# Attention: when the keys and values of the later blocks are asked for

## The chip, the cores and the metric

The kernel runs on one core of a Trainium2 chip. The metric is the device time of one launch in microseconds. Three runs of the kernel before took 2055.99, 2061.31 and 2060.2 us; their median is 2060.2 us.

The engines of a core work side by side, each through its own list of instructions in order: TensorE (PE) multiplies, VectorE (DVE), ScalarE (ACT) and GpSimd (POOL) do the elementwise work, SyncE (SP) mostly starts DMAs. They wait for each other by semaphores. An instruction that waits holds up all that stands behind it on its engine.

## The reference

One step of a two-layer encoder over 2048 prompt tokens and 32 sampled tokens, width 1024. The first layer is a gated delta rule, the second an attention with a sliding window over whole blocks of 64 tokens. Only the second is touched here:

```
proj = x @ w_in                                  # queries (16 heads of 64) and gates
q = rope(proj[:, :1024]) * 64 ** -0.5
kb, vb = band(k), band(v)                        # for each block: two blocks back and its own
s = einsum('bnqkgd,bnskd->bnkgqs', q, kb)        # 4 key heads, 4 query heads to each
s = where(key_chunk >= 0, s, -inf)
p = exp(s - m) / (sum(exp(s - m)) + exp(sink - m))   # m: the largest of the row and its sink
o = einsum('bnkgqs,bnskd->bnqkgd', p, vb)
out = layer_norm(alpha * x + (o * silu(z)) @ w_out)
```

Keys and values are one shared set, projected once from the output of the first layer. A block n reads the keys and values of blocks n-2, n-1 and n; block 0 reads one, block 1 two. The sampled tokens read a cache and their own keys.

## The kernel before, in words

The work of the last part: class P2 has projected keys, values, queries and gates for all tokens and has stored them in DRAM (scratch tensors `bk`, `bv`, `bq`, `bz`). Class Attention reads them back. Its loop `run` takes one block of 64 queries at a time, called a unit here; i counts the units. The order is blocks 8 to 31, then 0 to 7, then the sampled tokens, so unit i is block i + 8 for i below 24. It begins with block 8, since the projections of the last tokens are not done yet: their products (the generator `gates`, called by `fill`, two halves of a product at a time; lines 1714 to 1716) are mixed into the first units as filling work for PE.

A unit on PE is: products of probabilities with values (`values`, line 2098), the scores of the unit two ahead for one half of the heads (`scores`, line 2065), the transposes of the next unit's probabilities (line 2080), the output product of a finished pair of blocks (lines 1157 to 1159, weights `wo`), and the same for the other half of the heads. Between scores and transposes stand the maximum on DVE (line 1880), the exponentials on ACT (line 1885), the reciprocal on DVE (line 1889) and the product of the two on POOL (line 1899, tile P). The first output product is in unit 3, since a pair of blocks has to be finished first.

All keys lie in one tile `kT` (128 partitions, 2 x 2048 numbers: 16 KB a partition) and all values in one tile `vd` (two copies of 64 partitions for the two head halves). `load_keys(a, z)` is one DMA for blocks a to z - 1 (line 1847), `load_values(a, z)` two (line 1853). A block costs 64 KB of keys and 64 KB of values. Blocks 6 to 11 are loaded ahead of the loop, blocks 12 to 31 in step m = 4 of `gates`, which falls ahead of unit 0, and blocks 0 to 5 in `opened`, in unit 2.

In this stage the order on all five engines, SP's too, is written by hand (`manual_schedule` with PE, DVE, Activation, Pool and SP): what stands first in the program is issued first. On SP's list stand, beside the key and value loads: the last fetches of projection weights (line 1389), the rotary tables (1764), the stores of projected rows and gates (1747, 1740) and the regrouping of the rows (1751), the output weights `wo` in three parts (1826: four ahead of unit 0, one in unit 0, three in `opened`), the queries of a pair of blocks (`start`, line 2043, two DMAs), its gates (`gate`, 2048), the residual rows (1909) and the stores of the output (1962). From unit 4 on, each even unit has a `start`, a `gate`, a residual row and, when one is ready, an output store; odd units had no DMA.

Three places matter for the change: the loads in `gates` and in `opened`, and the top of the loop in `run`.

Of the kernel before, what the change touches and what calls it, by code (L numbers as in the profile page):

```python
# [36 lines left out]
def new_pool(tc, es, name, bufs=1, space=None, side=None):  # L37
    kw = {"reuse_waits": "tile"}
    if side is not None:
        kw["side"] = side  # L40
    if space is not None:
        kw["space"] = space
    return es.enter_context(tc.tile_pool(name=name, bufs=bufs, **kw))
# [49 lines left out]
def drain(gen):  # L93
    for _ in gen:
        pass
# [530 lines left out]
class Delta:  # L626
# [366 lines left out]
    LOADS = "Lk", "LE", "Lq0", "Lq1"  # L993
# [330 lines left out]
class P2:  # L1324
# [8 lines left out]
    FETCH, SUM, CAST, SUB, STEPS = 12, 5, 3, 2, 2  # L1333
    EARLY, LATE = 4, 2
    HELD, MORE = 5, 3
# [3 lines left out]
    def __init__(self, tc, right, front, spare, I, O, T, G):  # L1339
# [9 lines left out]
        self.ppr = new_pool(tc, spare, "p2_psr", 2, PSUM, side="right")  # L1349
        self.slots = self.EARLY + self.LATE  # L1350
        self.sub = self.nc.gpsimd
# [443 lines left out]
class Attention:  # L1795


    EARLY = 4
    LATE = 5

    def __init__(self, tc, left, I, O, T, G):
        self.tc, self.nc, self.I, self.O, self.T, self.G = tc, tc.nc, I, O, T, G
# [29 lines left out]
    def middle_weights(self, left):  # L1832
        return self.weights(new_pool(self.tc, left, "t_wo2", 1, side="left"), self.EARLY, self.LATE)

# [6 lines left out]
    def load_late(self):  # L1841
        drain(self.weights(self.oone, self.LATE, KC))
        yield
        self.tabs = ln_tables(self.nc.sync, self.oone, self.I["b_ln_g"], self.I["b_ln_b"])
# [270 lines left out]
    def run(self, gates, opened):  # L2115

        order = list(range(8, 32)) + list(range(8))
        last = len(order)
        P, pts, soft = {}, {}, {}
        gate = iter(gates)  # L2120

        def fill(n):
            for _ in range(n):
                next(gate, None)

        def score(i, p):
            if i <= last:
                P[i, p], soft[i, p] = self.scores(order[i], p) if i < last else self.sampled_scores(p)

        def sinks(i, p):  # L2130
            if i < last:
                self.place_sinks(p, 2, self.keys(order[i])[1] * 64, p * 4)
            elif i == last:
                self.place_sinks(p, 1, 160, 8 + 2 * p)

        def largest(i, p):
            if i <= last:
                self.largest(soft[i, p])

        def exps(i, p):  # L2140
            if i <= last:
                self.exps(soft[i, p])
                sinks(i + 1, p)

        def shares(i, p):
            if i <= last:
                x = soft.pop((i, p))
                self.inverse(x)
                self.shares(x)

        def turn(i, p):
            x = P.pop((i, p))
            pts[i, p] = self.turned(order[i], x) if i < last else self.sampled_turned(x)

        def copies(i, p):
            if i < last:
                self.copies(order[i], *pts[i, p])
            else:
                self.sampled_copies(*pts[i, p])

        def got(i):
            return [pts.pop((i, p))[0] for p in range(2)]

        norm = [None, None]

        def step(n):
            for _ in range(n if norm[1] else 0):
                next(norm[1], None)

        def early(i, p):  # L2170
            score(i, p)
            largest(i, p)
            exps(i, p)

        sinks(0, 0)
        sinks(0, 1)
        fill(4)
        early(0, 0)
        fill(2)
        shares(0, 0)  # L2180
        early(0, 1)
        fill(2)
        shares(0, 1)
        early(1, 0)
        turn(0, 0)
        copies(0, 0)
        fill(2)
        turn(0, 1)
        copies(0, 1)
        shares(1, 0)  # L2190
        score(1, 1)
        po = done = following = stored = None
        for i in range(last):
            c = (i + 1) % 2
            if i >= 3 and c == 0:
                done, po = po, following
            if i == 1:
                self.start(order[6])
            elif i == 2:
                self.gate(order[6])  # L2200
            elif i % 2 == 0:
                if i + 4 < last:
                    self.start(order[i + 4])
                    self.gate(order[i + 4])
                if i + 4 == last:
                    self.sampled_keys()
            if i == 2:
                fill(1)
            banks = self.values(order[i], got(i))
            gated = self.gated(order[i], banks, c)  # L2210
            largest(i + 1, 1)
            exps(i + 1, 1)
            drain(gated)
            score(i + 2, 0)
            turn(i + 1, 0)
            copies(i + 1, 0)
            largest(i + 2, 0)
            exps(i + 2, 0)
            shares(i + 1, 1)
            if i < 2:  # L2220
                fill(2)
            if po:
                self.product(po, c, 0)
            old = None
            if i >= 4:
                x = po if c else done
                if x:
                    self.stats(x, 1 - c)
                    if c == 0:
                        old = norm[0]  # L2230
                        step(20)
                        norm[:] = x, self.norm(x)
            step(4)
            shares(i + 2, 0)
            step(5)
            if c == 1 and i >= 2:
                following = self.finish(*self.pend.pop(0)) if i > 2 else opened()
                self.cast(following)
                self.rest(following)
            if old:  # L2240
                self.normed(old)
                self.affine(old)
                stored = old
            elif stored:
                self.store(stored)
                stored = None
            if po:
                self.product(po, c, 1)
                self.added(po, c)
            turn(i + 1, 1)  # L2250
            copies(i + 1, 1)
            score(i + 2, 1)
        self.store(stored)
        old = norm[0]
        step(20)
        self.normed(old)
        self.pend.append(self.sampled_values(got(last)))
        final, sampled = self.pend
        self.product(po, 1, 0)
        self.stats(po, 0)  # L2260
        some = self.finish(*sampled)
        self.cast(some)
        self.rest(some)
        self.affine(old)
        self.product(po, 1, 1)
        self.added(po, 1)
        self.stats(po, 1)
        end = self.finish(*final)
        self.cast(end)
        self.rest(end)  # L2270
        self.store(old)
        drain(self.norm(po))
        self.normed(po)
        self.affine(po)
        for c in range(2):
            self.product(some, c, 0)
            self.product(some, c, 1)
            self.added(some, c)
            self.stats(some, c)
        self.store(po)  # L2280
        for c in range(2):
            self.product(end, c, 0)
            self.product(end, c, 1)
            if c == 0:
                drain(self.norm(some))
                self.normed(some)
                self.affine(some)
                self.store(some)
            self.added(end, c)
            self.stats(end, c)  # L2290
        self.tail(end)
# [20 lines left out]
def program(tc, I, O, T, G):  # L2312
# [108 lines left out]
    att = Attention(tc, left, I, O, T, G)  # L2421
    later.append(att)

    def gates():
        for m in range(14):
            next(p2.main)
            next(p2.main)
            if m == 4:
                att.load_keys(12, 32)
                att.load_values(12, 32)  # L2430
                early = att.early_weights()
            elif m == 6:
                next(early)
            elif m == 8:
                drain(early)
            elif m == 10:
                front.close()
                drain(att.middle_weights(left))
            yield
        drain(p2.main)  # L2440
        p2.finish_all()
        yield

    def opened():
        right.close()
        att.open_right(right)
        late_weights = att.load_late()
        next(late_weights)
        first = att.finish(*att.pend.pop(0))
        drain(late_weights)  # L2450
        att.load_keys(0, 6)
        att.load_values(0, 6)
        return first

    with tc.manual_schedule(engines={ET.PE, ET.DVE, ET.Activation, ET.Pool, ET.SP}):
# [165 lines left out]
```

## Time and profile before

| | |
|---|---|
| median of three runs | 2060.2 us (2055.99 to 2061.31) |
| the profiled execution | 2062.93 us, its span 2061.1 us |
| PE busy | 1998.8 us, 97% of the span |
| PE weight loads busy | 1826.2 us (beside the products) |
| DVE, ACT, POOL busy | 1471.9, 1000.2, 748.0 us |
| DMA | 377.85 MB, 183 GB/s on average |

A profile is one execution. A row of the timeline gives the start in us, the length, engine, line, operation, the tiles written and read, how many were merged, and in brackets the idle time of the engine ahead of it and who ended that. "SPq" rows are SP's issues of DMAs: their length is the time that SP needs to hand the DMA over, not that of the transfer. A row of a window gives the stretch, its length, busy time of PE, PE's weight loads, DVE, ACT and POOL (number of instructions in brackets), the granted clock of PE, the busy share of the 16 DMA engines (it can go above 1, since packets overlap) and GB/s.

### The profile page before, as it was taken

The numbers are of one execution on the slowest core, as the hardware profiler recorded it, in microseconds if no ns is written. First come the engines' busy times: TensorE is split into PE (matmuls) and PEld (weight loads), VectorE is DVE, ScalarE is ACT, GpSimd is POOL, SyncE is SP. The second block draws the span as 40 slices with busy tenths as digits, with TensorE's granted clock in tenths as the row PEclk, the third lists the DMA queues.
The fourth block names the chain that finished last, engine by engine and source line by source line (L and its number), as shares of the span: only waits on it lengthen the run. The fifth ranks groups of instructions, "written<-read, shape, count | busy, mean of one in ns | idle before, by whom it ended". The sixth has DMA issues, their size and how long they took to land. (4 is left out here: it accounts for less than half of the span.)

```text
span 2061.1 us, 36534 instructions
## 1 busy us (share of the span) xinstructions
PE 1998.8 (97%) x13246; PEld 1826.2 (89%) x13246; DVE 1471.9 (71%) x2701; ACT 1000.2 (49%) x2437; POOL 748.0 (36%) x1151
## 2 busy tenths in 40 slices
PE   8999999999999999999889999899999998999998
PEld 6999999999999999999788887799999996777775
DVE  4567656677666778888987998777777654666665
ACT  4354444436632277777763222534643435555552
POOL 0412112112223258888860123022000023566665
PEclk9999999999999999999999999999999999999999
DMA  5134255447878566666884989888768579433321
GB/s 211 48 116 126 72 128 124 104 97 207 208 164 242 152 202 217 197 206 196 299 277 131 268 254 255 279 259 298 259 200 247 184 225 310 121 103 103 103 74 67
DMA packets 477077, 377.85 MB, mean 183 GB/s; under 512 B 291024, under 2 KB 397808, under 8 KB 476880
## 3 DMA queue, kind: packets, MB, share of 16 engines
q1 hardware_dynamic: 437136, 356.88, 57.7%
q10 hardware_dynamic: 39760, 18.64, 3.4%
q8 instruction: 104, 1.70, 0.3%
q14 instruction: 77, 0.63, 0.1%
HBM read 244.06 MB, written 142.58 MB: 188 GB/s over the span
## 5 line engine op out<-in xcount | busy, mean ns | idle before, releaser
L79 PE MATMUL ps<-act_hi,w_hi 128*128 128x416 f32 x1280 | 455.7, 356 | 4.0 <-DVE z L579 3.7
L81 PE MATMUL ps<-act_hi,w_lo 128*128 128x416 f32 x1280 | 450.5, 353 | 0.0
L80 PE MATMUL ps<-act_lo,w_hi 128*128 128x416 f32 x1280 | 448.9, 351 | 0.0
L79 PEld LDWEIGHTS ps<-act_hi,w_hi 128*128 128x128 f32 x1280 | 240.8, 188 | 9.3 <-DVE z L579 4.0
L81 PEld LDWEIGHTS ps<-act_hi,w_lo 128*128 128x128 f32 x1280 | 240.6, 188 | 3.8
L80 PEld LDWEIGHTS ps<-act_lo,w_hi 128*128 128x128 f32 x1280 | 241.1, 188 | 3.0
L212 DVE SCALAR_TENSOR_TENSOR y<-R,convw,y 128x2083 f32<-128x2083 f32 x72 | 175.5, 2438 | 57.5 <-ACT y L209 46.5
L56 POOL TENSOR_TENSOR w_lo<-w_raw,w_hi 128x1024 fp32r<-128x1024 f32 x25 | 72.3, 2891 | 275.7 <-ACT w_hi L55 275.1
L755 POOL TENSOR_TENSOR tm<-L,Tt 128x60 f32<-128x60 f32 (+19 forms) x365 | 134.8, 369 | 73.2 <-issue 43.0
L1885 ACT ACTIVATE e<-S,nm 128x193 f32<-128x193 f32 (+2 forms) x260 | 104.8, 416 | 102.8 <-DVE nm L1880 62.0
L757 POOL TENSOR_TENSOR Tt<-Tt,tm 128x60 f32<-128x60 f32 (+19 forms) x365 | 140.0, 383 | 28.6
L1899 POOL TENSOR_TENSOR P<-e,sm 128x384 f32<-128x384 f32 (+2 forms) x128 | 102.5, 823 | 123.4 <-DVE sm L1889 117.3
L326 ACT COPY R<-ps 128x416 f32<-128x416 f32 (+1 forms) x144 | 59.7, 445 | 125.5 <-PE ps L81 119.9
L1542 ACT ACTIVATE o<-X 128x416 f32<-128x416 f32 x80 | 41.5, 519 | 144.8 <-PE X L1716 141.6
L1383 POOL TENSOR_TENSOR wo_parts<-wo_parts 128x512 fp32r<-128x512 f32 x16 | 21.4, 1341 | 240.8 <-ACT wo_parts L1703 240.8
L1157 PE MATMUL ot<-wo,g_hi 128*128 128x512 f32 x256 | 103.9, 406 | 1.8 <-DMA wo<-s_wob 1.8
L1383 DVE TENSOR_TENSOR w_lo<-w_raw,w_hi 128x512 fp32r<-128x512 f32 x134 | 95.8, 729 | 7.7 <-ACT w_hi L1395 5.9
L1158 PE MATMUL ot<-wo,g_hi 128*128 128x512 f32 x256 | 100.8, 394 | 0.0
L1159 PE MATMUL ot<-wo,g_lo 128*128 128x512 f32 x256 | 100.8, 394 | 0.0
L1430 POOL TENSOR_TENSOR act_raw<-act_raw 128x416 f32<-128x416 f32 x32 | 40.0, 1250 | 126.5 <-DMA act_raw<-s_hT 124.7
L1395 ACT CAST w_hi<-w_raw 128x512 fp32r<-128x512 f32 x129 | 76.2, 614 | 7.7 <-DVE r L1165 6.1
L218 DVE SCALAR_TENSOR_TENSOR y<-th,y 128x2083 f32<-128x2083 f32 x24 | 55.8, 2327 | 33.1 <-ACT th L216 33.1
(368 smaller groups left out, 5076.8 us busy)
## 6 DMA issues: line engine op xcount, KB each, us to landing
w_raw<-in_b_w SPq DMA_DIRECT2D x60, 512.0 KB
w_raw<-in_w_in SPq DMA_DIRECT2D x40, 512.0 KB
act_raw<-s_hT SPq DMA_DIRECT2D x64, 208.0 KB
s_rows<-o SPq DMA_DIRECT2D x50, 208.0 KB
k<-s_k SPq DMA_DIRECT2D x17, 512.0 KB
E<-s_E SPq DMA_DIRECT2D x17, 512.0 KB
s_bq<-s_rows SPq DMA_DIRECT2D x40, 208.0 KB
s_bz<-o SPq DMA_DIRECT2D x40, 208.0 KB
```

Source lines behind the costliest of these rows:

```text
L79: nc.tensor.matmul(ps, hi[:, k, :], xh[:, k, :], start=(k == 0), stop=False)
L80: nc.tensor.matmul(ps, hi[:, k, :], xl[:, k, :], start=False, stop=False)
L81: nc.tensor.matmul(ps, lo[:, k, :], xh[:, k, :], start=False, stop=(k == KC - 1))
L212: nc.vector.scalar_tensor_tensor(out=y[:], in0=R[:, j:j + W], scalar=self.convw[:, i, j:j + 1], in1=y[:], op0=ALU.mult, op1=ALU.add)
L755: P.tensor_tensor(out=tm[:n, i0 - k:, :w], in0=L[:n, i0:, j:j + 1].to_broadcast(sh), in1=Tt[:n, j:j + 1, :w].to_broadcast(sh), op=ALU.mult)
L757: P.tensor_tensor(out=Tt[:n, i0:, :w], in0=Tt[:n, i0:, :w], in1=tm[:n, i0 - k:, :w], op=ALU.subtract)
L1157: nc.tensor.matmul(ps[:n], ghi[:, k, :n], hi, start=a, stop=False)
L1158: nc.tensor.matmul(ps[:n], ghi[:, k, :n], lo, start=False, stop=False)
L1159: nc.tensor.matmul(ps[:n], glo[:, k, :n], hi, start=False, stop=z)
L1383: P.tensor_tensor(out=lo, in0=raw, in1=hi, op=ALU.subtract)
L1885: self.nc.scalar.activation(x.e[:, h, u, :x.n], x.S[:, h, u, :], AF.Exp, bias=x.nm[:, h, u:u + 1], scale=1.0, accum_out=x.sm[:, h, u:u + 1])
L1899: self.nc.gpsimd.tensor_tensor(out=x.P[:, u, :nj * 128].rearrange("r (j h k) -> r j h k", h=2, k=64), in0=x.e[:, :, u, :n].rearrange("r h ...
```

## The change

Blocks 12 to 31 are no longer loaded together ahead of unit 0; only blocks 12 to 15 are. Blocks 16 to 19 are asked for at the top of unit 3, blocks 20 to 25 at the top of unit 5, blocks 26 to 31 at the top of unit 9, and blocks 0 to 5, which were loaded in unit 2, at the top of unit 13. The loads are the same functions with other bounds: 15 DMAs in place of 6 for the same 3,328 KB. Keys and values of a block are needed first by the scores two units ahead of its own unit: block 16 in unit 6, block 20 in unit 10, block 26 in unit 16, block 0 in unit 22.

```diff
     EARLY = 4
     LATE = 5
+    LOADS = {3: (16, 20), 5: (20, 26), 9: (26, 32), 13: (0, 6)}
...
             if i >= 3 and c == 0:
                 done, po = po, following
+            if i in self.LOADS:
+                self.load_keys(*self.LOADS[i])
+                self.load_values(*self.LOADS[i])
             if i == 1:
                 self.start(order[6])
...
             if m == 4:
-                att.load_keys(12, 32)
-                att.load_values(12, 32)
+                att.load_keys(12, 16)
+                att.load_values(12, 16)
                 early = att.early_weights()
...
         drain(late_weights)
-        att.load_keys(0, 6)
-        att.load_values(0, 6)
         return first
```

## The prediction

> **What bounds the kernel now.** I read the span and the busy time by stretches first, then every idle gap of TensorE (PE) in the stretch that has any, then the queue of SyncE (SP), which issues all the loads of this stage, and what the DMA engines moved.
>
> ```profile
> span 2061.1 us, 36534 instructions
> ...
> 1680.00:1750.00 70.00, 63.07 (x454) 50.43 (x453) 36.98 (x69) 31.61 (x120) 26.84 (x32) 0.95 1.00 311
> 1750.00:2050.00 300.00, 300.00 (x2133) 228.16 (x2132) 183.53 (x479) 150.93 (x523) 191.98 (x155) 1.00 0.35 97
> ```
>
> Columns of the last two: stretch in us, its length, busy time of PE, PE's weight loads, VectorE (DVE), ScalarE (ACT) and GpSimd (POOL), then PE's granted clock, the DMA engines' busy share and GB/s. The attention stage starts near 1680. From 1750 to 2050 PE is busy in all 300.00 us at full clock with the DMA engines at 0.35: there nothing but PE sets the end, and a load can only do harm. From 1680 to 1750 PE idles 70.00 - 63.07 = 6.93 us, and the DMA engines are full (1.00). Whatever this change wins, it wins in those 70 us. Their gaps, in the timeline (in brackets the idle time before the row, and who ended it):
>
> ```profile
> 1690.43 0.46 PE L1716 MATMUL ot<-act_hi,w_lo 128*128 128x416 f32 x1 [1.51 <-DVE w_lo L1383]
> ...
> 1705.13 0.33 PE L2080 MATMUL tr<-ident,P 128*128 128x128 f32 x1 [0.24 <-POOL P L1899]
> ...
> 1705.92 0.77 PE L2080 MATMUL tr<-ident,P 128*128 128x128 f32 x5 [0.46 <-POOL P L1899]
> ...
> 1727.62 0.48 PE L2080 MATMUL tr<-ident,P 128*128 128x128 f32 x1 [2.60 <-POOL P L1899]
> ...
> 1728.41 1.33 PE L2080 MATMUL tr<-ident,P 128*128 128x128 f32 x5 [0.31 <-POOL P L1899]
> ...
> 1740.07 0.50 PE L1157 MATMUL ot<-wo,g_hi 128*128 128x512 f32 x1 [0.21 <-DMA wo<-s_wob]
> ...
> 1742.63 0.50 PE L1157 MATMUL ot<-wo,g_hi 128*128 128x512 f32 x1 [1.60 <-DMA wo<-s_wob]
> ```
>
> Four stalls: A 1.51, B 0.24 + 0.46 = 0.70, C 2.60 + 0.31 = 2.91, D 0.21 + 1.60 = 1.81; together 6.93, all of the idle time. The question is which of them hang on the big load of keys and values.
>
> **The change part by part.** *The load at the begin.* Blocks 12 to 32 of the keys and values are one group of three DMAs, between stalls A and B:
>
> ```profile
> kT<-s_bk SPq DMA_DIRECT2D x1, 1280.0 KB
> vd<-s_bv SPq DMA_DIRECT2D x2, 640.0 KB
> ```
> ```profile
> 1685.32 0.38 SPq L1847 DMA_DIRECT2D kT<-s_bk  x1
> 1686.63 5.07 SPq L1853 DMA_DIRECT2D vd<-s_bv  x2
> 1691.80 4.70 SPq L1747 DMA_DIRECT2D s_rows<-o  x1
> 1696.59 0.38 SPq L1389 DMA_DIRECT2D w_raw<-in_b_w  x1
> ...
> 1701.89 0.33 SPq L1740 DMA_DIRECT2D s_bz<-o  x1
> 1702.33 10.30 SPq L2043 DMA_DIRECT2D qs<-s_bq  x2
> ...
> 1725.37 1.30 SPq L1740 DMA_DIRECT2D s_bz<-o  x2
> 1731.11 1.40 SPq L1826 DMA_DIRECT2D wo<-s_wob  x3
> ```
> ```profile
> 1688.00:1694.00 6.00, 4.49 (x27) 3.87 (x24) 5.96 (x12) 2.13 (x9) 1.27 (x2) 1.00 1.04 393
> 1694.00:1700.00 6.00, 6.00 (x39) 5.46 (x38) 5.50 (x9) 4.10 (x18) 5.29 (x7) 1.00 1.23 183
> ```
> ```profile
> SPq L1740 <- DMA vd<-s_bv: 1.9, 1, 1.9
> ```
>
> An issue lasts 0.38 us when the queue takes it at once; 4.70 and 10.30 us mean that SP stands until the DMA engines have drained. The engines move 393 GB/s in 1688 to 1694 and 183 GB/s in 1694 to 1700 at a share of 1.23: I read the first as the keys and the second as mostly the values, whose pieces are 512 bytes (128 floats a token) against 5 KB a partition row for the keys. The wait of L1740 on the values ended at its issue at 1701.89, so the values, asked for by 1691.7, had landed only then. Queue time of the group: 1.31 MB / 393 GB/s = 3.3 us and 1.31 MB / 183 GB/s = 7.2 us, 10.5 in all. Four of twenty blocks stay; the other four fifths, 8.4 us of queue time, go out of this stretch.
>
> *Stall B.* What was behind the group: the row store, and then the last weight fetch.
>
> ```profile
> 1690.30 0.58 DVE L1777 TENSOR_TENSOR o<-o 128x416 f32<-128x416 f32 x1
> ...
> 1702.24 0.17 DVE L1889 RECIPROCAL sm<-sm 128x4 f32<-128x4 f32 x1
> ```
> ```profile
> 1703.67 0.62 POOL L1395 CAST w_hi<-w_raw 128x512 fp32r<-128x512 f32 x1 [3.42 <-DMA w_raw<-in_b_w]
> 1704.25 1.62 POOL L1899 TENSOR_TENSOR P<-e,sm 128x384 f32<-128x384 f32 x2
> ```
>
> The store's operand is done at 1690.88 (the first row), so without backpressure it goes at about 1691.2 and the weight fetch at about 1691.7 instead of 1696.59, and no values stand ahead of it: with the same 7.1 us from issue to cast it is there by 1698.8 rather than 1703.67. POOL casts it in its free time, and the shares P start when their reciprocal is there (1702.41) instead of at 1704.25, 1.8 us earlier. B needs 0.70: it goes. Value taken **-0.70**, bounds -0.70 and 0.
>
> *Stall D.* The last three output weights are issued at 1731.11. That issue follows the landing of the last gate stores, whose buffers they take over:
>
> ```profile
> 1726.21 4.76 DMA s_bz<-o
> ```
> ```profile
> 1721.58 1.08 DVE L1738 SCALAR_TENSOR_TENSOR o<-o 128x416 f32<-128x416 f32 x2
> ```
> ```profile
> 1714.00:1731.00 17.00, 14.09 (x108) 11.34 (x104) 8.26 (x18) 10.73 (x40) 7.28 (x9) 0.88 0.92 255
> ```
>
> The data of those stores is ready at 1722.66, but the second goes out at 1726.2: SP was held up before by the full queue (the 10.30 us above) and works through queries, gates and regroupings late. With 8.4 us less ahead, SP is back with the engines by then: stores at about 1722.7 less the 0.70 of B, landed within 4.76 us, weights asked for by 1727 instead of 1731.1. PE reaches them 0.70 earlier too, so D goes when they come 1.81 + 0.70 = 2.51 us earlier; 4 us are in hand. Value taken **-1.81**, bounds -1.81 and 0 (SP could be held by something on PE's own time).
>
> *Stalls A and C.* The loads that A waits for were issued before 1685.32. Value 0; if later DMAs share the engines with earlier ones, up to -1.51. C is the way from scores over maximum, exponentials, reciprocal and POOL's shares to the transpose at a place where the filling products have run out; no DMA is in it. Value 0. It has a tail in the clock:
>
> ```profile
> 1726.00:1728.00 2.00, 0.38 (x1) 0.18 (x1) 0.57 (x2) 1.42 (x7) 1.26 (x2) 0.74 0.89 288
> 1728.00:1730.00 2.00, 1.69 (x8) 1.26 (x9) 0.40 (x2) 1.67 (x4) 1.60 (x3) 0.50 0.97 322
> 1730.00:1732.00 2.00, 2.00 (x16) 1.37 (x18) 0.96 (x2) 0.00 (x0) 2.00 (x2) 0.50 0.09 34
> 1732.00:1734.00 2.00, 2.00 (x22) 0.81 (x14) 0.34 (x1) 1.57 (x8) 0.68 (x1) 0.55 0.75 201
> ```
>
> Busy time times missing clock is 0.38 x 0.26 + 1.69 x 0.50 + 2.00 x 0.50 + 2.00 x 0.45 = 2.8 us. I keep it in the sum (value 0) and make its absence a rival.
>
> *The three later groups and the one that changes place.* In unit 3, blocks 16 to 20 (512 KB) stand where blocks 0 to 6 (768 KB) stood, a little cheaper. Units 5, 9 and 13 get three DMAs each, nine more issues of 0.4 us or a little more on SP, about 5 us, in a stretch where SP waits far longer for DVE alone and the DMA engines are idle for most of the time:
>
> ```profile
> SPq L2048 <- DVE graw L2109: 77.4, 10, 11.4
> ```
> ```profile
> 1762.00:1950.00 188.00, 188.00 (x1406) 144.27 (x1405) 116.38 (x300) 99.81 (x358) 120.94 (x101) 1.00 0.36 99
> ```
> ```profile
> 1766.89 0.92 PE L2065 MATMUL S<-kT,qs 64*128 64x192 f32 x8
> ```
>
> That row is the end of unit 6, the first scores on block 16 (unit 6 scores two units ahead): some 30 us after the load's issue near 1735. A unit lasts about 10 us (1733.93, quoted below, is in unit 3); the others have five units or more, over 50 us. Query, gate and residual loads behind them on SP move back by at most one group's time: 0.39 MB / 393 + 0.39 MB / 183 GB/s = 3.1 us, against a lead of about two units (20 us). Cover gone, a late group would cost PE those 3.1 us. First readers get a few more semaphores to pass: bounds 0 and 0.3, taken **+0.1**.
>
> The Trainium skill, "DMA: Bandwidth & Descriptors", section "Rules for kernel authors", speaks against the change twice: one large transfer rather than many, and a DMA issued early with the wait put late. By its table (64 KB at 138, 1 MB at 341 GB/s) a 256 KB piece would as an estimate take 0.8 to 1.9 us, and with the engines at a share of 0.36 the sum stays as it is; the rows here show in 1685 to 1731 what asking early costs the others.
>
> **The sum.** The profiled execution took 2062.93 us (span 2061.1). -0.70 - 1.81 + 0.1 = -2.4, so 2060.5 for it; it lies 2.7 above the median of the runs, 2060.2, and for the median the same saving gives **2057.8**.
>
> **The rivals.** *Only B goes*: SP reaches the last stores no earlier, because something on PE's own time holds it. For it: two of the stores end at 1722.66 only. Against: SP's long issues. 2060.2 - 0.6 = 2059.6. With B staying as well, 2060.3.
>
> *The clock does not fall.* C stays, but a shift of 0.7 us or more moves it against whatever decides on the clock: the idle of A left it at 1.00 (the row of 1688 to 1694), that of C did not. 2057.8 - 2.8 = 2055.0. The Trainium skill, "TensorE: Matmul & The Clock Gate", section "What's actually happening", says that the gate looks at free-running windows of about 3.4 us; the trace agrees in size (about two such windows at 0.50), and it would make the fall a matter of phase, different from run to run.
>
> *More goes*: A as well and the clock too, 2055.0 - 1.5 = 2053.5.
>
> *Slower: loads and scores lock each other.* If a load into one part of kT counted as a write of all of it, each of the four loads in the units would wait for the last scores, and the next scores for its landing. Landing takes about 4.76 us (the row above); 24 value products (about 1.5 us) lie between. The price is 4 x 3.3 = 13 us, and more with the clock; with 4.4 each, 2057.8 + 17.6 = 2075. It decides as soon as a landing takes over 1.5 us. The trace of before speaks against it:
>
> ```profile
> 1687.43 0.92 PE L2065 MATMUL S<-kT,qs 64*128 64x192 f32 x8
> ...
> 1733.93 0.92 PE L2065 MATMUL S<-kT,qs 64*128 64x192 f32 x8
> ```
> ```profile
> 1734.60 0.43 SPq L1847 DMA_DIRECT2D kT<-s_bk  x1
> ```
>
> The scores of 1733.93 come after the load of blocks 0 to 6 in the program and ran before it was even issued; those of 1687.43 ran 2.1 us after the load of 12 to 32, ahead of its landing.
>
> **How the numbers follow.** Forecast 0.52; only B or nothing 0.22; the clock does not fall 0.15; more 0.05; slower 0.06. 0.3% is 6.2 us, about what a measurement can tell here (the three runs spread over 5.3). Faster than 2054.0 are "more" and the lower part of the clock's case, spread over the runs' scatter: 0.11. Slower than 2066.4: the lock, 0.06. The rest, 0.83, is no difference. The range, 2053.0 to 2062.0, goes from a little under "more" to a little above "nothing"; outside lie the lock and the scatter's ends.
>
> **What would show it.** Right: the values' issue at 1686 takes about 1.2 us instead of 5.07, the row store under 1, the queries' 10.30 less than half; POOL's cast has no wait on the weight fetch; no PE gap before L2080 near 1705; the last weights asked for before 1728.6 and no gap before L1157; C with its 2.9 us; PE busy throughout after 1750. Wrong: a gap that ends in kT or vd after 1750; D still there with the stores on time; A gone; PE idle in 1680 to 1750 above 6.93 us.

## The result and the profile after

The kernel after takes 2056.13 us in the median, the kernel before 2060.32 beside it; the ratio is 0.9973, with a 95% interval of 0.9961 to 0.9986, so 2.9 to 8.0 us less. Measured a second time, the same two kernels gave 0.9986 [0.9970, 1.0002].

The stretches of the profile after (columns as in the prediction), with the page's span ahead of them:

```profile
span 2052.9 us, 36545 instructions
...
1680.00:1742.00 62.00, 56.86 (x420) 46.09 (x419) 37.71 (x69) 31.42 (x121) 27.45 (x32) 0.94 0.96 302
1742.00:2042.00 300.00, 300.00 (x2133) 228.12 (x2132) 183.34 (x479) 150.70 (x522) 192.00 (x155) 1.00 0.38 102
```

The idle gaps of PE in it, from its timeline:

```profile
1684.92 0.46 PE L1716 MATMUL ot<-act_hi,w_lo 128*128 128x416 f32 x1 [2.08 <-DVE w_lo L1383]
...
1722.68 0.33 PE L2081 MATMUL tr<-ident,P 128*128 128x128 f32 x1 [2.60 <-POOL P L1900]
...
1723.47 1.03 PE L2081 MATMUL tr<-ident,P 128*128 128x128 f32 x5 [0.46 <-POOL P L1900]
```

These are A, now 2.08 us, and C, 2.60 + 0.46 = 3.06; together 5.14 = 62.00 - 56.86, all of the idle time. B and D are gone. In the 300 us behind, PE is busy throughout at full clock: none of the later loads holds it up. (Line numbers from 1800 on are one higher here.) The queue of SP, from the first key load of the stage on:

```profile
1659.89 0.39 SPq L1848 DMA_DIRECT2D kT<-s_bk  x1
...
1679.81 0.38 SPq L1848 DMA_DIRECT2D kT<-s_bk  x1
1681.10 1.25 SPq L1854 DMA_DIRECT2D vd<-s_bv  x2
1685.40 0.33 SPq L1747 DMA_DIRECT2D s_rows<-o  x1
1686.00 0.34 SPq L1389 DMA_DIRECT2D w_raw<-in_b_w  x1
...
1695.58 5.47 SPq L2044 DMA_DIRECT2D qs<-s_bq  x2
1717.25 0.83 SPq L1740 DMA_DIRECT2D s_bz<-o  x2
1720.98 1.40 SPq L1827 DMA_DIRECT2D wo<-s_wob  x3
```

The values are handed over in 1.25 us instead of 5.07, the row store in 0.33 instead of 4.70, the queries in 5.47 instead of 10.30. The weight fetch behind the row store is there when POOL wants it; the cast has no wait in brackets:

```profile
1693.65 2.00 POOL L1395 CAST w_hi<-w_raw 128x512 fp32r<-128x512 f32 x2
```

**The spans mustn't be subtracted as they are.** They differ by 2061.1 - 2052.9 = 8.2 us, but the first key load of the attention stage (blocks 6 to 11), which stands ahead of all that changed, was issued 6.1 us earlier after than before (1659.89 above). That row in the profile of before, and in a second profile of the very kernel after:

```profile
1665.98 0.39 SPq L1847 DMA_DIRECT2D kT<-s_bk  x1
```
```profile
1668.33 0.39 SPq L1848 DMA_DIRECT2D kT<-s_bk  x1
```

The engines' orders ahead of it are the same in all these kernels, and over all profiles of this study it lies between 1656.4 and 1668.3: scatter of what runs before. So I compare the **stage**, the span less that time: 395.1 us before, 393.0 and 392.7 in the two profiles after. From the first value products of unit 4 on, every kernel below but one needs 316.1 to 316.3 us to the end, so all differences lie in the first four units and just ahead of them.

### The profile page after: what moved, and what is told of

Read it like the earlier page. It is cut to its first block, busy times and chain, and to the rows that moved or that the text cites. A ratio compares the mean times of both kernels' runs of the same rounds, so it can differ in the third digit from the quotient of the medians.

```text
span 2052.9 us, 36545 instructions
## 1 busy us (share of the span) xinstructions
PE 1999.1 (97%) x13246; PEld 1829.3 (89%) x13246; DVE 1482.7 (72%) x2701; ACT 1000.2 (49%) x2437; POOL 739.8 (36%) x1151
## 5 line engine op out<-in xcount | busy, mean ns | idle before, releaser
L56 POOL TENSOR_TENSOR w_lo<-w_raw,w_hi 128x1024 fp32r<-128x1024 f32 x25 | 62.8, 2513 | 277.4 <-ACT w_hi L55 277.4
```

## The experiments

My theory was the prediction's: the big group fills SP's queue, which makes the last weight fetch (B) and the last output weights (D) late. The rivals: the gain lies in where the loads stand later; or in the change of place of blocks 0 to 5; or it is scatter between two builds. The edits are against the kernel after. Stage, stalls and clock come from one profile of each kernel; the ratio comes from 6 to 12 runs of it and 12 to 35 of the kernel before. The half-clock column says after which stall the granted clock fell and for how long: the missing clock of the windows of 2 us, added up, times 2 us, divided by 0.5. In the profile of before, 0.26 + 0.50 + 0.50 + 0.45 = 1.71 gives 6.8 us behind C.

| kernel | stage | A / B / C / D, us idle | half clock, us | ratio to before [95%] |
|---|---|---|---|---|
| before | 395.1 | 1.51 / 0.70 / 2.91 / 1.81 | C 6.8 | |
| same | 397.7 | 1.87 / 0 / 3.06 / 2.88 | A 3.4, C 3.4, D 3.4 | 0.9999 [0.9988, 1.0010] |
| only_zero | 397.4 | 2.07 / 0 / 3.06 / 2.32 | A 3.4, C 3.4, D 3.4 | 1.0005 [0.9992, 1.0018] |
| all_front | 398.4 | 1.63 / 4.25 / 3.05 / 0 | B 3.4, C 6.8 | 1.0007 [0.9994, 1.0020] |
| after | 393.0 | 2.08 / 0 / 3.06 / 0 | A 3.4, C 3.4 | 0.9973 [0.9961, 0.9986] |
| after_again | 392.7 | 1.83 / 0 / 3.06 / 0 | A 3.4, C 3.4 | 0.9986 [0.9970, 1.0002] |
| keys_front | 394.3 | 2.01 / 0 / 2.96 / 0 | A 3.4, C 6.8 | 0.9980 [0.9969, 0.9991] |
| values_front | 394.3 | 2.02 / 0 / 2.92 / 0 | A 3.4, C 6.8 | 0.9983 [0.9971, 0.9995] |
| unit3 | 394.8 | 1.47 / 0 / 3.06 / 1.25, and 2.46 later | 3.4 late | 0.9989 [0.9978, 1.0000] |
| gates_behind | 389.1 | 0 / 0 / 3.06 / 0 | C 3.4 | 0.9964 [0.9950, 0.9977] |
| whole_gates_behind | 397.4 | 0 / 5.30 / 3.06 / 0 | B 3.4, C 6.8 | 1.0004 [0.9991, 1.0016] |
| scores_first | 388.9 | 0 / 0 / 2.13 / 0 | C 3.4 | 0.9965 [0.9954, 0.9977] |

### same and after_again: the two kernels once more

`after_again` is the kernel after without an edit; `same` has its lines with the loads of before:

```diff
-    LOADS = {3: (16, 20), 5: (20, 26), 9: (26, 32), 13: (0, 6)}
+    LOADS = {}
...
-                att.load_keys(12, 16)
-                att.load_values(12, 16)
+                att.load_keys(12, 32)
+                att.load_values(12, 32)
...
-        drain(late_weights)
+        drain(late_weights); att.load_keys(0, 6); att.load_values(0, 6)
```

> The kernel before with shifted line numbers: a second look at the same program, for the scatter. Theory (the gain lies in the first four units): ratio 1.000 within 0.15%; from the first load of keys (blocks 6 to 12) to the end 395 us as in the first profile, within 3 us for the clock; the four stalls 1.5, 0.7, 2.9 and 1.8 us again; the time ahead of that load differs by several us from the first profile's 1666. Rival (the 6 us ahead of the attention stage by which the two profiles differ belong to the change): that load again near 1666 and never near 1660.

> The changed kernel unchanged. Theory: ratio 0.9975 to 0.9985 of the kernel before (3 to 5 us); from the first load of keys to the end 391 to 393.5 us; no stall at the transposes of unit 0 and none before the output weights; the load itself anywhere from 1658 to 1668, as it is scatter. Rival (the change also speeds up what lies ahead): the load near 1660 again.

Measured: 0.9999 [0.9988, 1.0010] and 0.9986 [0.9970, 1.0002]. The profile of `same` is the more telling of the two. Three rows of PE, two waits and the transposes behind them, after the row of A:

```profile
1685.62 0.46 PE L1716 MATMUL ot<-act_hi,w_lo 128*128 128x416 f32 x1 [1.87 <-DVE w_lo L1383]
...
1735.95 0.50 PE L1157 MATMUL ot<-wo,g_hi 128*128 128x512 f32 x1 [1.28 <-DMA wo<-s_wob]
...
1738.52 0.79 PE L1157 MATMUL ot<-wo,g_hi 128*128 128x512 f32 x1 [1.60 <-DMA wo<-s_wob]
1739.96 1.48 PE L2081 MATMUL tr<-ident,P 128*128 128x128 f32 x6
```

Its clock, in two stretches:

```profile
1687.00:1690.00 3.00, 3.00 (x11) 2.85 (x10) 2.96 (x7) 0.81 (x4) 1.47 (x2) 0.53 1.07 329
...
1735.00:1742.00 7.00, 4.44 (x18) 3.24 (x20) 1.21 (x2) 0.48 (x1) 0.82 (x2) 0.76 1.01 378
```

A is 1.87 here and is followed by half clock (0.53), PE comes later to the first transposes, and B isn't there, although POOL waits for the weights as before:

```profile
1698.71 0.62 POOL L1395 CAST w_hi<-w_raw 128x512 fp32r<-128x512 f32 x1 [3.29 <-DMA w_raw<-in_b_w]
```

D is 1.28 + 1.60 = 2.88, and the clock falls behind it: 0.24 x 7.00 / 0.5 = 3.4 us. So the one profile on which the prediction rests was the odd one of three: the same loads give stages of 395.1 there, 397.7 here and 397.4 in the next kernel. The mean of the three is 396.7, that of the two profiles after 392.85: **3.9 us less**, and the ratios agree with it (0.9973 and 0.9986 are 5.6 and 2.9 us).

### only_zero: blocks 0 to 5 alone change their place

```diff
-    LOADS = {3: (16, 20), 5: (20, 26), 9: (26, 32), 13: (0, 6)}
+    LOADS = {13: (0, 6)}
...
-                att.load_keys(12, 16)
-                att.load_values(12, 16)
+                att.load_keys(12, 32)
+                att.load_values(12, 32)
```

> Only blocks 0 to 6 are moved to unit 13; blocks 12 to 32 at the begin as before. Theory: they stood behind the last output weights in the queue, so nothing changes: stall before the output weights 1.8 to 2.9 us as in the two profiles of before, 395 to 398 us from the first load of keys to the end, ratio 0.9990 to 1.0010. Rival (the load of unit 2 shares the engines with the output weights ahead of it): that stall 1 us or more shorter, ratio 0.9985 or less.

Measured: 1.0005 [0.9992, 1.0018]; that part of the change brings nothing. D is there as in `same`:

```profile
1736.18 0.50 PE L1157 MATMUL ot<-wo,g_hi 128*128 128x512 f32 x1 [0.72 <-DMA wo<-s_wob]
...
1738.74 0.76 PE L1157 MATMUL ot<-wo,g_hi 128*128 128x512 f32 x1 [1.60 <-DMA wo<-s_wob]
```

### all_front: everything ahead of unit 0

```diff
-    LOADS = {3: (16, 20), 5: (20, 26), 9: (26, 32), 13: (0, 6)}
+    LOADS = {}
...
-                att.load_keys(12, 16)
-                att.load_values(12, 16)
+                att.load_keys(12, 32); att.load_keys(0, 6)
+                att.load_values(12, 32); att.load_values(0, 6)
```

> The other way: blocks 0 to 6 are asked for at the begin too, with 12 to 32. Theory (what the group costs the weights behind it is queue time): 3.1 us more ahead of the last weight fetch and of the queries; their issue stands 13 us instead of 10.3, the stall at the transposes of unit 0 grows to 2 to 4 us, the one before the output weights stays at 1.5 to 3; from the first load of keys to the end 397 to 400 us against 395.1 and 397.7 in the two profiles of before; ratio 1.000 to 1.002. Rival (the two stalls do not hang on the group): as before, no stall longer.

Measured: 1.0007 [0.9994, 1.0020]. The first part of the chain came out as the theory has it. SP's values, POOL's cast and PE's transpose:

```profile
1677.84 11.34 SPq L1854 DMA_DIRECT2D vd<-s_bv  x4
...
1698.00 0.61 POOL L1395 CAST w_hi<-w_raw 128x512 fp32r<-128x512 f32 x1 [7.13 <-DMA w_raw<-in_b_w]
...
1699.45 0.48 PE L2081 MATMUL tr<-ident,P 128*128 128x128 f32 x1 [3.94 <-POOL P L1900]
```

B has grown to 3.94 + 0.31 = 4.25 us. The queries' issue, for which I had expected 13 us, took 8.71: more of the wait fell on the values' own issue. The second part did not come: I had D stay, and it is 0. Counted from the first key load, the last weights are asked for 3.2 us later than before (68.3 against 65.1), but PE, held up in B and by the half clock behind it, begins the output product 5.3 us later (74.8 against 69.4), and the weights are there when it needs them. **Two stalls behind one queue don't add up; the earlier one pays for the later one.** That is why six more blocks in front cost hardly more than the twenty did.

### keys_front and values_front: which of the loads

```diff
-                self.load_keys(*self.LOADS[i])
+                self.load_keys(*self.LOADS[i]) if i == 13 else None
...
-                att.load_keys(12, 16)
+                att.load_keys(12, 32)
```

`values_front` is the same edit on the values, with the keys in four parts.

> The change for the values alone: keys of blocks 12 to 32 are asked for at the begin as before, values in four parts. Theory (the values, in 512 byte pieces, are the slow part: 7.2 of 10.5 us of queue time): 5.8 of the 8.4 us relief remain, so both stalls (0.7 at the transposes of unit 0, 1.8 before the output weights) are gone or the second is under 0.5, and the time is that of the whole change within 0.1%. Rival (bytes alone count): half of the relief, 4.2 us, so the weights come about 2 us earlier than before and about 0.5 us or more of the second stall stays, the same here as in values_front.

> The change for the keys alone: values of blocks 12 to 32 at the begin as before, keys in four parts. Theory (values are the slow part): relief of 2.6 us of queue time only; the weight cast of POOL comes at about 1.5 to 2 us earlier against the units, so the stall at the transposes goes, while 0.5 to 1.8 us of the stall before the output weights stay; 0.5 to 2 us slower than the whole change. Rival (bytes alone count): the same as keys_front.

Measured: 0.9980 [0.9969, 0.9991] and 0.9983 [0.9971, 0.9995]. On PE they are alike: B and D gone in both, stage 394.3 in both. I had expected that with the values in front part of D would stay; it doesn't, so half of the relief is enough on PE. On the queue they differ as the prediction's reading of keys and values says. The queries' issue and a stretch in which the DMA engines move the group, for the keys in front:

```profile
1691.99 5.00 SPq L2044 DMA_DIRECT2D qs<-s_bq  x2
```
```profile
1681.70:1684.40 2.70, 2.70 (x9) 2.57 (x8) 2.67 (x8) 1.17 (x5) 0.16 (x1) 0.50 1.01 411
```

and for the values in front:

```profile
1697.06 8.69 SPq L2044 DMA_DIRECT2D qs<-s_bq  x2
```
```profile
1689.00:1691.00 2.00, 2.00 (x10) 1.93 (x9) 2.00 (x5) 0.88 (x5) 1.68 (x2) 0.74 1.23 179
1691.00:1693.00 2.00, 2.00 (x16) 1.67 (x14) 1.49 (x2) 1.80 (x7) 1.86 (x3) 1.00 1.23 198
```

1.05 MB more of keys leave the queries' issue at 5.00 us (5.47 after), as much of values brings it to 8.69, with the engines at 179 to 198 GB/s and a share of 1.23. The values are the slow part, at about half the keys' 411 GB/s (the prediction's 393 comes from a stretch in which other fetches ran too). Their pieces are short (512 bytes), and each of their DMAs writes only 64 partitions. The short pieces alone don't explain it: in `whole_gates_behind`, below, two loads of gates follow the values, also in pieces of 512 bytes, but into all 128 partitions. The values' stretch and the gates', told apart by the order of the queue and the number of packets:

```profile
1686.00:1692.00 6.00, 6.00 (x38) 5.46 (x37) 5.50 (x9) 4.25 (x18) 4.83 (x6) 1.00 1.23 186
1693.00:1695.00 2.00, 2.00 (x23) 1.51 (x25) 0.98 (x3) 0.89 (x2) 0.00 (x0) 1.00 1.21 290
```

186 GB/s against 290. The half set of partitions and the order of the values in DRAM remain as possible causes; no kernel here parts these two.

### unit3: all the later blocks in one group in unit 3

```diff
-    LOADS = {3: (16, 20), 5: (20, 26), 9: (26, 32), 13: (0, 6)}
+    LOADS = {3: (16, 32)}
...
-        drain(late_weights)
+        drain(late_weights); att.load_keys(0, 6); att.load_values(0, 6)
```

> Blocks 16 to 32 in one group at the top of unit 3, blocks 0 to 6 in unit 2 as before: the begin is cut as in the change, but the rest isn't spread. Theory (only the cut at the begin counts): no stall after unit 3, 392.5 to 394.5 us from the first load of keys to the end, the time of the whole change within 0.1%. Rival (the spread counts): the 11.5 us of queue time behind the output weights make queries, gates or residual rows of units 4 to 6 late: a stall of over 1 us there and a time 1 to 4 us above that of the change.

Measured: 0.9989 [0.9978, 1.0000]; the stage is 394.8, about 2 us above that of the kernel after, and it is the one kernel that needs more than that from unit 4 on (320.1). Its SP, DVE and PE:

```profile
1732.53 6.24 SPq L1854 DMA_DIRECT2D vd<-s_bv  x2
...
1750.42 1.29 SPq L1910 DMA_DIRECT2D r<-s_h  x1
```
```profile
1756.99 0.69 DVE L1165 SCALAR_TENSOR_TENSOR r<-r,ot 128x512 f32<-128x512 f32 x1 [4.07 <-DMA r<-s_h]
```
```profile
1732.42 0.50 PE L1157 MATMUL ot<-wo,g_hi 128*128 128x512 f32 x1 [1.25 <-DMA wo<-s_wob]
...
1757.73 2.84 PE L2099 MATMUL ot<-pt,vd 64*64 64x256 f32 x24 [2.46 <-DVE r L1165]
```

The big group does in unit 3 what it did ahead of unit 0: SP stands in its issue, what is asked for behind it comes late (here the residual row that is asked for in unit 4), and PE stands 2.46 us for DVE, with half clock behind. So the spread over several units counts, not just the removal from the front; this rests on the profile, since the ratios of whole runs (0.9989 here, 0.9973 and 0.9986 for the kernel after) don't part the two. The D of 1.25 tells something else: neither A (1.47) nor C was followed by half clock in this profile, so PE began the output product 65.9 us behind the first key load (69.6 in the kernel after), and the weights, asked for at the same time (60.8 against 61.1), weren't all there yet.

### gates_behind and whole_gates_behind: what was left, A

A waits on DVE, which has waited for a rotary table; the regrouped gates of units 0 and 2 are fetched ahead of that table. `gates_behind` fetches them behind the keys and values; `whole_gates_behind` is the same move on the kernel before.

```diff
-                att.load_values(12, 16)
+                att.load_values(12, 16); att.gate(8); att.gate(10)
...
         att.load_values(6, 12)
         att.start(10)
-        att.gate(8)
-        att.gate(10)
```

> The whole change, and the gates of the first two pairs of blocks (1 MB in 512 byte pieces) are asked for behind the cut group of keys and values instead of ahead of the last rotary tables and weights. Theory (the stall of about 2 us in the products ahead of unit 0 is queue time too, of what stands ahead of the tables): it goes, and with it the 3.4 us at half clock behind it; up to 0.8 us may come back at the transposes of unit 0; 389 to 390.5 us from the first load of keys to the end, 2.5 to 3.7 us under the change, ratio 0.996 to 0.9975. Rival (the tables wait for the weight fetches ahead of them): the stall stays above 1 us and the time is that of the change.

> The kernel before with the gates of the first two pairs asked for behind the whole group of keys and values. Theory (the stall ahead of unit 0 and the one at its transposes hang on one queue: as long as the group is whole, taking the first away lets PE arrive earlier at the second): the stall of 1.5 to 2.1 us ahead of unit 0 goes, the one at the transposes of unit 0 becomes 2 to 4 us, the one before the output weights stays at 1.5 to 3; 395 to 397.5 us from the first load of keys to the end; ratio 0.9988 to 1.0005. Rival (the gates' place pays for itself, with or without the cut): the gain of gates_behind over the change, about 3.7 us, comes here too: ratio 0.9975 to 0.9985.

Measured: 0.9964 [0.9950, 0.9977], 2051.77 us in the median, and 1.0004 [0.9991, 1.0016]. The table's wait on DVE in the kernel after, and in `gates_behind`:

```profile
1682.31 0.59 DVE L1771 TENSOR_TENSOR o<-o 128x416 f32<-128x416 f32 x1 [9.81 <-DMA o<-in_cs]
```
```profile
1683.58 0.59 DVE L1771 TENSOR_TENSOR o<-o 128x416 f32<-128x416 f32 x1 [6.41 <-DMA o<-in_cs]
```

All that PE waits for in the first units of `gates_behind` (us in total, times, longest) is C:

```profile
PE tr L2081 <- POOL P L1900: 3.1, 2, 2.6
```

A and the half clock behind it are gone, and the stage falls from 392.85 to 389.1. The size is that of one profile: the ratio, of six runs, has an interval that overlaps that of the kernel after. On the kernel before the same move takes A away too and gains nothing:

```profile
1700.31 0.61 POOL L1395 CAST w_hi<-w_raw 128x512 fp32r<-128x512 f32 x1 [8.77 <-DMA w_raw<-in_b_w]
...
1701.77 0.33 PE L2081 MATMUL tr<-ident,P 128*128 128x128 f32 x1 [4.84 <-POOL P L1900]
```

There the gates stand behind the whole group in the queue and the weight fetch behind both; B grows to 5.30, and D goes for the reason seen in `all_front` (I had expected it to stay). The move is worth something only with the short group.

### scores_first: less of C

On top of `gates_behind`, PE does the second half of unit 4's scores ahead of the last transposes of unit 3 instead of behind them, which gives it something to do in C:

```diff
+            score(i + 2, 1) if i == 2 else None
             turn(i + 1, 1)
-            copies(i + 1, 1)
-            score(i + 2, 1)
+            copies(i + 1, 1); score(i + 2, 1) if i != 2 else None
```

> gates_behind, and in unit 2 alone the scores of the unit two ahead (second half of the heads) come before the transposes that wait for POOL's shares, instead of behind them. Theory (the 2.6 us stall in unit 2 is a place without filling work, and the half clock hangs on the length of one idle stretch): 0.85 us of products go into it, the idle time there falls from 3.1 to 2.1 to 2.4 us, and the 3.4 us at half clock behind it may go as well: 0.7 to 0.9 us without the clock, 2 to 2.6 with it; 386.5 to 388.4 us from the first load of keys to the end, ratio 0.9950 to 0.9962. Rival (the scores wait for ACT to read the bank first, and push the transposes back by as much): no gain, 389 us.

Measured: 0.9965 [0.9954, 0.9977], stage 388.9 against 389.1, so 0.2 us where at least 0.7 was expected. The gaps, and what follows them:

```profile
1723.65 0.92 PE L2066 MATMUL S<-kT,qs 64*128 64x192 f32 x8 [0.37 <-ACT e L1886]
...
1725.88 0.33 PE L2081 MATMUL tr<-ident,P 128*128 128x128 f32 x1 [1.30 <-POOL P L1900]
...
1726.66 0.77 PE L2081 MATMUL tr<-ident,P 128*128 128x128 f32 x5 [0.46 <-POOL P L1900]
...
1727.36 3.33 PE L2099 MATMUL ot<-pt,vd 64*64 64x256 f32 x24
1730.62 1.31 PE L2066 MATMUL S<-kT,qs 64*128 64x192 f32 x8
```

The same two kinds of rows in `gates_behind`:

```profile
1726.00 2.84 PE L2099 MATMUL ot<-pt,vd 64*64 64x256 f32 x24
1728.77 0.97 PE L2066 MATMUL S<-kT,qs 64*128 64x192 f32 x8
```

C has shrunk from 3.06 to 0.37 + 1.30 + 0.46 = 2.13 us. But the clock still falls for 3.4 us, now over other work: the values take 3.33 instead of 2.84, the next scores 1.31 instead of 0.97. That is 0.83 of the 0.93 us given back.

## Why the prediction was right, and where it was not

**The sign and the mechanism held. The saving was larger than forecast: 3.9 us in the stage, 2.9 to 8.0 in the first measurement of whole runs, where the sum said 2.4. One term was mis-sized, and one gain wasn't typical.**

*Stall B, -0.70.* The steps ahead of it are as forecast: counted from the first key load, the weight fetch is issued at 26.1 us instead of 30.6, and its cast waits for nothing. But the 0.70 is worth less than that. Both other profiles with the whole group (`same`, `only_zero`) have no B at all, because a longer A with half clock behind it makes PE late. It was there in one execution of three. All five profiles with the whole group in front fit this: B is there in the three without half clock behind A (`before`, `all_front`, `whole_gates_behind`) and absent in the two with it.

*Stall D, -1.81.* This is the mis-sized term. The way to it is right: the last weights are asked for 61.1 us behind the first key load instead of 65.1, 4.0 earlier, where the prediction had 4.1. But D was 1.81, 2.88 and 2.32 us in the three profiles with the whole group, 2.3 in the mean, and in two of them the clock fell behind it for 3.4 us, up to 1.7 us of time, which the sum left out. The "4 us in hand" were too much on the other hand: with no fall behind A and C (`unit3`) 1.25 us of D came back.

*Stall A, 0, and stall C, 0.* Both right: A is 1.82 in the mean of the three and 1.96 in the two after, C 3.01 and 3.06. Over all four stalls the idle time goes from 7.40 to 5.02 us, 2.4 less. That this is the sum's own figure is luck: B counted 0.5 us too much there and D 0.5 too little. Of the remaining 1.5 us of the 3.9, the clock can account for up to 1.1: half clock was 6.8, 10.2 and 10.2 us, and is 6.8 in both profiles after, 2.3 us less on average. How much of that is chance, three profiles against two can't say.

*The clock behind C.* Kept in the sum at 2.8 us and made a rival; it still falls in every profile but one, for 3.4 or 6.8 us, whatever the loads are. Nothing in these runs ties it to the loads; what it does follow is in the last section.

*The added waits, +0.1, and the later groups.* PE is busy in 300.00 of 300 us behind; the lock between loads and scores, the slower rival, did not show. "Only B goes" is refuted by D, which went in every kernel with a shorter group in front but `unit3`; "more goes" by A, which stayed until the gates were moved.

*What was to show it.* All of it is there but one: the queries' issue of 5.47 us is a little more than half of 10.30.

## What to carry to other kernels

A load that is far from its first use costs nothing at its own place and something at every place behind it in the queue: look for issues that last several us, list what stands behind them, and ask whether an engine waits for that. Stalls behind one queue trade off against each other, so price them together and in a second profile of the same kernel before you call one of them a gain. When one queue entry has been moved away, try the next one in front of the remaining stall: the gates' fetch brought about as much again in the stage, and nothing without the first step.

## What the runs showed of the hardware

Behind the stalls of this stage the granted clock fell in whole stretches: 3.4 or 6.8 us at 0.50, nothing between. These rows of the kernel after show one, after C:

```profile
1722.00:1724.00 2.00, 0.85 (x5) 0.67 (x6) 0.18 (x1) 2.00 (x9) 1.60 (x3) 0.96 0.87 227
1724.00:1726.00 2.00, 2.00 (x11) 1.25 (x9) 0.56 (x1) 0.69 (x2) 2.00 (x3) 0.50 0.99 381
1726.00:1728.00 2.00, 2.00 (x26) 1.08 (x24) 0.96 (x1) 0.81 (x5) 1.74 (x1) 0.69 1.01 403
```

0.04 + 0.50 + 0.31 = 0.85, times 2 us, divided by 0.5, is 3.4 us. The Trainium skill, "TensorE: Matmul & The Clock Gate", section "What's actually happening", gives a free-running window of 3.413 us; the length agrees. What brings the fall on does not agree with its advice, in "Why this matters for your kernels", to keep idle gaps below about 3 us: at A, idle times of 1.47, 1.51 and 1.63 us were followed by full clock, and 1.83 us and more by half clock each time; C's 3.06 was once (`unit3`) followed by none, and 2.13 us in three pieces by one. A gap that is a third shorter can cost just as much.

The place of a stall counts beside its length. In one profile the falls begin whole multiples of 3.413 us apart by the trace's clock records (1686.29 and 1723.84 us in the kernel after: 11 of them), so the time ahead of a fall can be divided into windows of that length. In the twelve profiles, 23 windows of these stalls at full clock held 1.72 us or more of idle PE, and 22 of them were followed by half clock (the exception is 1.76 in `whole_gates_behind`); none that held 1.63 or less was. A window's idle time is its length less PE's busy time, the first number behind the comma. C in `unit3` falls on two windows, with 1.49 and 1.57 us:

```profile
1716.25:1719.66 3.41, 1.92 (x22) 1.26 (x14) 2.54 (x6) 2.09 (x9) 0.00 (x0) 1.00 0.95 308
1719.66:1723.08 3.42, 1.85 (x14) 1.29 (x14) 0.80 (x3) 3.04 (x10) 2.79 (x4) 1.00 0.27 49
```

The shorter C of `scores_first` lies mostly in one, with 1.7 us, and half clock follows:

```profile
1724.61:1728.03 3.42, 1.69 (x14) 0.96 (x18) 0.96 (x5) 3.04 (x10) 2.64 (x4) 1.00 0.37 67
```

No experiment moved a stall against the windows on purpose. But where the stalls fall on the windows differs from profile to profile, and D hangs on that: in `unit3`, where the clock had stayed up, PE reached the output weights early enough to wait for them.

What stays open: why the time ahead of the attention stage scatters by 12 us at the same order of instructions, what makes a fall last two windows, and which of the two remaining causes makes the values slow.
